# The relu of an index score stays in its PSUM bank, and a convolution is summed in a PSUM bank

## Chip, cores and metric

The kernel runs on one core of one Trainium2 chip. The metric is the device time of one execution in microseconds, the median of the runs shown.
The engines of the core are named as in the profile: PE (TensorE, matmuls), PEld (its weight loads), DVE (VectorE), ACT (ScalarE), POOL (GpSimd) and SP (which only issues DMAs here).
Each has its own list of instructions, fixed when the kernel is built, and runs it in that order: an instruction that waits holds up all that stand behind it on its engine.

## What is computed

The reference is a decoder of two layers over 512 tokens of width 1024, in fp32. Each layer has a mixer of four head groups (HGRN2, DSA, NSA, mLSTM), a cross attention and a SwiGLU. The change touches two places.

DSA's index picks 128 keys for each query by a score that sums relu'd products over eight heads:

```
rel = relu(einsum('bthd,bsd->bhts', iqb, ik))
score = einsum('bhts,bth->bts', rel, iwb)
score = where(causal, score, -inf);  _, idx = top_k(score, topk)
```

mLSTM's queries and keys come from a causal convolution of four taps along the tokens, and a silu:

```
qk = silu(causal_conv(qk, conv_w, conv_b));  q, k = split(qk, 2)
```

## The kernel before

Activations stand with features or tokens on the 128 partitions and 512 or fewer columns in the free dimension. Every fp32 matmul against a weight is made of three (high times high, low times high, high times low: L294 to L296 and L304 to L306). The weights come by DMA from SP into `wr`, ACT rounds them to `wh` (L285) and POOL subtracts to `wl` (L286, a two-input subtraction over 128x512).

A layer has three stages, and each opens its own PSUM banks. In the first, which the change is in, the banks are `acc` (two, from a pool that lives throughout), `tp`, `dt`, `o` and `mb` (one each) and `sc` (two). The first stage weaves together generators: DSA's index and selection (`dsa`), NSA (`nsa`, which mixes its attention and its compressed branch `nsa_cmp`), mLSTM (`ml`) and the input projections. Each `yield` gives a cost, and the shares in `COST` set in which order the instructions are recorded; a scheduler then sets the order on each engine by a timeline of its own. The order is thus not written in the code, and any change of buffers can move instructions that it does not name.

DSA's index, for each block of 128 queries from the second on (`tb` 1 to 3): two rounds of transposes give `iqT` (L458, in bank `dt`), and for each of eight heads a matmul writes scores into bank `dt` (L644; the alias maps `sc` and `tp` of this pool to `dt`), ACT writes the relu to an SBUF tile `rel` of a tag with four buffers (L646), and DVE adds it, times the head's weight, to `iacc` in SBUF (L649 and L650 for the first head, L653 for the others). `iacc` has one buffer. Sixteen rounds of MAX8 and MATCH_REPLACE8 (L661, L662) then select the 128 best in place, and L665 turns the result into a mask.

Bank `dt` has a single buffer and is shared with `nsa_cmp`: the transposes of `n_hid` (L1165), the product with `hT` (L1173), and others go through it.

mLSTM's convolution of one 128-feature chunk (`conv`) is an ACT instruction that writes tap 0 and the bias to `m_y` (L971), three DVE instructions that each add a tap (L973; inputs `m_x` and `m_y`, both in SBUF), a tanh on ACT (L975), the product of the silu on DVE (L977) and a split in high and low (L980 on ACT, then `m_lo` on POOL). It is called four times in a layer. Bank `mb` serves mLSTM's transposes (L957, and L458 with `mb`), its scores (L1013) and its values (L1030).

`nsa_cmp` runs twice over the same steps, once for keys and once for values: DVE gathers `n_blk` (L1145), adds the positions, splits it into `n_bs` (L1150 and a subtraction at the helper's line L316), and PE multiplies `n_bs` with 64 streamed weights (L1157) into an `acc` bank.

Of the kernel before, what the change touches and what calls it, by code (L numbers as in the profile page):

```python
# [15 lines left out]
D, S, MEM, DEPTH, FF = 1024, 512, 256, 2, 2816  # L16
# [186 lines left out]
class Kernel:  # L203
# [403 lines left out]
    def dsa(self, pool, keep):  # L607
        nc = self.nc
        idx = self.d_idx
        st = self.t(pool, "d_st", [128, 64], bufs=1)  # L610

        ik = idx[:, :, 256:288]
        self.sumsq(st[:, 4:8], ik, pool)
        self.rsqrt(pool, st[:, 8:12], st[:, 4:8], 1.0 / 32, EPS)
        self.tt(ik, ik, st[:, 8:12, None].to_broadcast([128, TB, 32]), OP.mult)
        self.tt(ik, ik, self.row("idxk_gain")[:, None, :].to_broadcast([128, TB, 32]), OP.mult)
        self.rope(idx[:, :, 256:288].rearrange("p t (h d) -> p t h d", h=1), self.ic, self.isn, 4, pool)
        iq = idx[:, :, 0:256].rearrange("p t (h d) -> p t h d", h=8)
        self.rope(iq, self.ic, self.isn, 4, pool)
        iks = self.t2(pool, "iks", [128, TB, 96], FR)  # L620
        nc.vector.tensor_copy(iks[:, :, 0:32], ik)
        nc.vector.tensor_copy(iks[:, :, 32:64], ik)
        self.tt(iks[:, :, 64:96], ik, iks[:, :, 0:32].bitcast(FT), OP.subtract)
        ikT = self.t(pool, "ikT", [128, S], FR, bufs=1)
        self.transpose_blocks(ikT[0:96], lambda j: iks[:, j, :].bitcast(FT), TB, nc.vector.tensor_copy, rows=96,
                              pool=pool)

        yield 4.0

        def index(tb):  # L630
            n = (tb + 1) * 128
            iqs = self.t(pool, "iqs", [128, 8, 96], FR, bufs=1)
            nc.scalar.activation(iqs[:, :, 0:32], iq[:, tb], AF.Copy)
            nc.scalar.activation(iqs[:, :, 64:96], iq[:, tb], AF.Copy)
            self.tt(iqs[:, :, 32:64], iq[:, tb], iqs[:, :, 0:32].bitcast(FT), OP.subtract, nc.gpsimd)
            iqT = self.t(pool, "iqT", [128, 8, 128], FR, bufs=1)
            for g in range(2):
                self.transpose_blocks(iqT[0:96, 4 * g:4 * g + 4].rearrange("p a b -> p (a b)"),
                                      lambda j: iqs[:, 4 * g + j, :].bitcast(FT), 4, self.act_copy, rows=96,
                                      pool=pool)  # L640
            acc = self.t(pool, "iacc", [128, S], bufs=1)[:, :n]
            for h in range(8):
                sc = self.psum("sc", pool=pool)
                nc.tensor.matmul(sc[:, :n], iqT[0:96, h], ikT[0:96, :n], start=True, stop=True)  # L644
                rel = self.t2(pool, "rel", [128, S])
                nc.scalar.activation(rel[:, :n], sc[:, :n], AF.Relu, scale=1.0 / 16)  # L646
                w = idx[:, tb, 288 + h:289 + h]
                if h == 0:
                    nc.vector.tensor_scalar(acc[:, :n - 128], rel[:, :n - 128], w, None, op0=OP.mult)  # L649
                    nc.vector.scalar_tensor_tensor(acc[:, n - 128:n], rel[:, n - 128:n], w, self.k("neg"),  # L650
                                                   op0=OP.mult, op1=OP.add)
                else:
                    nc.vector.scalar_tensor_tensor(acc, rel[:, :n], w, acc, op0=OP.mult, op1=OP.add)  # L653
                yield 0.7
            return acc

        def select(tb, acc, masks):
            n = (tb + 1) * 128
            m8 = self.t(pool, "m8", [128, 8])
            for r in range(16):  # L660
                nc.vector.max(m8, acc)  # L661
                nc.vector.match_replace(acc, m8, acc, -3e38)  # L662
                yield 0.4 + 0.25 * tb
            masks[tb] = self.t(keep, f"dmask{tb}", [128, n], BF, bufs=1)
            nc.vector.tensor_scalar(masks[tb], acc, -2e38, NEG, op0=OP.is_gt, op1=OP.mult)  # L665

        masks = self.d_masks = {0: None}
        for tb in range(1, TB):
            acc = yield from index(tb)
            yield from select(tb, acc, masks)  # L670
# [262 lines left out]
    def ml(self, pool):  # L933
# [33 lines left out]

        def conv(c):
            x = self.m_x[c]
            y = self.t2(pool, "m_y", [128, S])  # L970
            nc.scalar.activation(y, x[:, 0:S], AF.Identity, scale=self.col("conv_w", 4 * c), bias=self.col("conv_b", c))  # L971
            for j in range(1, 4):
                nc.vector.scalar_tensor_tensor(y, x[:, j:j + S], self.col("conv_w", 4 * c + j), y, op0=OP.mult, op1=OP.add)  # L973
            th = self.t2(pool, "m_th", [128, S])
            nc.scalar.activation(th, y, AF.Tanh, scale=0.5)  # L975
            z = th
            nc.vector.scalar_tensor_tensor(z, th, 1.0, y, op0=OP.add, op1=OP.mult)  # L977
            hi = self.t(pool, f"m_hi{c // 2}", [128, S], FR, bufs=1)
            lo = pool.tile([128, S], FR, name="m_lo", tag="m_x", bufs=4)
            nc.scalar.activation(hi, z, AF.Copy)  # L980
            self.tt(lo, z, hi.bitcast(FT), OP.subtract, nc.gpsimd)
            return hi, lo
# [10 lines left out]
        for h in range(4):  # L993
            po = 64 * (h % 2)
            if h % 2 == 0:
                while h and self.m_have < 2:
                    yield 0.2
                q = conv(h // 2)
                yield 3.0
                k = conv(2 + h // 2)  # L1000
                yield 3.0
# [6 lines left out]
            for sb in range(TB):  # L1008
                n = S - sb * 128
                sc = self.psum("mb")  # L1010
# [580 lines left out]
```

## Time and profile before

| what | value |
|---|---|
| median of 3 runs | 1689.46 us (1688.78 to 1691.2) |
| profiled execution | 1689.36 us, span 1687.6 us |
| mean granted TensorE clock | 0.973 of full speed |
| busy share of the span | PE 95%, PEld 79%, DVE 56%, POOL 47%, ACT 42% |
| first stage of layer 0 | from about 45 to 273 us |
| first stage of layer 1 | from about 884 to 1109 us |

The span begins with the first profiled instruction; 1.8 us of the execution lie outside it. Times in the text without another word are microseconds from the span's start in the profiled execution. A share of busy time is a mean over stages with different limits, so the stage of the change is read by itself.

### The profile page before, as it was taken

How to read it: one execution, taken by the hardware profiler on the slowest of the kernel's cores; microseconds unless marked ns; L12 is line 12 of the kernel's file. 1: busy time of each engine (PE TensorE's matmuls, PEld its weight loads, DVE VectorE, ACT ScalarE, POOL GpSimd, SP SyncE). 2: the span in 40 equal slices, each digit the busy share in tenths (PEclk: the TensorE clock that was granted, in tenths of full speed). 3: DMA queues.
4: the chain of work that ended last, by engine and by line, in shares of the span. 5: the costliest groups of instructions: out<-in, count | busy, mean ns of one | idle time of the engine just before them, and what ended most of it. 6: DMA issues, size and time to landing. Idle time of an engine off the chain costs nothing.

```text
span 1687.6 us, 25172 instructions
## 1 busy us (share of the span) xinstructions
PE 1608.2 (95%) x9256; PEld 1332.0 (79%) x9262; DVE 948.3 (56%) x1760; ACT 716.8 (42%) x1525; POOL 788.6 (47%) x698
## 2 busy tenths in 40 slices
PE   7899998998899999999998999889988999999999
PEld 7778877777788888888897787687867888888887
DVE  5697588875854421443227975887677644124420
ACT  5555453455653322333345654534555433223321
POOL 6554333456424444444456634244562344444442
PEclk9999997999999999999999999979999999999999
DMA  5342212213313333333232412022131233333332
GB/s 166 84 119 76 70 34 84 57 42 94 92 45 94 93 91 98 94 95 98 87 113 80 122 57 76 27 94 60 33 116 39 66 98 89 92 100 94 93 104 66
DMA packets 83259, 140.40 MB, mean 83 GB/s; under 512 B 9528, under 2 KB 24632, under 8 KB 83136
## 3 DMA queue, kind: packets, MB, share of 16 engines
q1 hardware_dynamic: 80784, 133.81, 27.2%
q10 hardware_dynamic: 2032, 3.94, 0.7%
q8 instruction: 73, 1.20, 0.3%
q0 software_dynamic: 320, 1.05, 0.2%
q14 instruction: 50, 0.41, 0.1%
HBM read 134.55 MB, written 4.21 MB: 82 GB/s over the span
## 4 chain that ended last, share of the span: by engine, by line
PE 79%; DVE 13%; issue 3%; ACT 2%; POOL 2%; DMA 1%; ACTq 0%; SPq 0%; POOLq 0%; DVEq 0%
PE acc L294 13%; PE acc L295 13%; PE acc L296 13%; PE sc L295 5%; PE sc L296 5%; PE sc L294 5%; PE hb L821 3%; PE acc L304 2%; PE acc L305 2%; PE acc L306 2%; PE o L539 2%; PE sc L517 2%; PE tp L458 2%; DVE m_y L973 1%; DVE iacc L662 1%
## 5 line engine op out<-in xcount | busy, mean ns | idle before, releaser
L286 POOL TENSOR_TENSOR wl<-wr,wh 128x512 fp32r<-128x512 f32 (+5 forms) x504 | 631.9, 1260 | 686.2 <-ACT wh L285 657.2
L285 ACT ACTIVATE wh<-wr 128x512 fp32r<-128x512 f32 (+5 forms) x504 | 297.1, 597 | 502.9 <-PE acc L295 209.9
L295 PE MATMUL acc<-xl,wh 128*128 128x512 f32 (+1 forms) x704 | 275.6, 392 | 3.3 <-DVE xl L1242 3.0
L294 PE MATMUL acc<-xh,wh 128*128 128x512 f32 (+1 forms) x704 | 276.3, 395 | 1.6 <-ACT xh L1248 1.1
L296 PE MATMUL acc<-xh,wl 128*128 128x512 f32 (+1 forms) x704 | 275.3, 391 | 2.5 <-POOL wl L286 2.5
L431 DVE TENSOR_TENSOR xT<-acc,xT 128x512 f32<-128x512 f32 (+1 forms) x112 | 68.0, 611 | 220.9 <-PE acc L296 220.3
L294 PEld LDWEIGHTS acc<-xh,wh 128*128 128x128 f32 x704 | 133.9, 191 | 34.0 <-DVE xT L431 2.1
L295 PEld LDWEIGHTS acc<-xl,wh 128*128 128x128 f32 x704 | 134.1, 190 | 32.2 <-DVE xl L1242 4.1
L296 PEld LDWEIGHTS acc<-xh,wl 128*128 128x128 f32 x704 | 134.1, 191 | 30.1 <-POOL wl L286 3.4
L304 PE MATMUL acc<-wh,xh 128*128 128x256 f32 (+2 forms) x480 | 139.8, 294 | 1.0 <-DVE xT L431 1.0
L305 PE MATMUL acc<-wl,xh 128*128 128x256 f32 (+2 forms) x480 | 138.3, 289 | 1.5 <-POOL wl L286 1.4
L295 PE MATMUL sc<-xl,wh 128*128 128x512 f32 x352 | 139.7, 397 | 0.0
L296 PE MATMUL sc<-xh,wl 128*128 128x512 f32 x352 | 138.9, 394 | 0.0
L296 PE MATMUL acc<-f_gh,wl 128*128 128x512 f32 x352 | 138.5, 395 | 0.0
L295 PE MATMUL acc<-f_gl,wh 128*128 128x512 f32 x352 | 138.4, 395 | 0.0
L294 PE MATMUL acc<-f_gh,wh 128*128 128x512 f32 x352 | 138.1, 394 | 0.0
L294 PE MATMUL sc<-xh,wh 128*128 128x512 f32 x352 | 138.0, 393 | 0.0
L306 PE MATMUL acc<-wh,xl 128*128 128x256 f32 (+2 forms) x480 | 136.9, 286 | 0.0
L1450 DVE SCALAR_TENSOR_TENSOR f_b<-sc,R 128x512 f32<-128x512 f32 x44 | 30.4, 690 | 127.5 <-PE sc L296 127.5
L304 PEld LDWEIGHTS acc<-wh,xh 128*128 128x128 f32 x480 | 91.9, 192 | 4.6 <-issue 2.1
L305 PEld LDWEIGHTS acc<-wl,xh 128*128 128x128 f32 x480 | 92.6, 193 | 3.0 <-POOL wl L286 2.0
L306 PEld LDWEIGHTS acc<-wh,xl 128*128 128x128 f32 x480 | 92.3, 192 | 0.1
(405 smaller groups left out, 3068.8 us busy)
## 6 DMA issues: line engine op xcount, KB each, us to landing
wr<-in_wst SPq DMA_DIRECT2D x384, 256.0 KB, 2.6
wr<-in_wst SPq DMA_DIRECT2D x48, 128.0 KB, 2.1
wr<-in_wst SPq DMA_DIRECT2D x32, 192.0 KB, 2.4
wr<-in_wst SPq DMA_DIRECT2D x16, 262.0 KB, 2.7
wr<-in_wst SPq DMA_DIRECT2D x16, 148.0 KB, 2.2
wr<-in_wst SPq DMA_DIRECT2D x8, 264.0 KB, 2.9
m_Mb<-m_dram ACTq DMA_DIRECT2D x8, 256.0 KB, 3.3
memT<-in_memT SPq DMA_DIRECT2D x16, 128.0 KB, 2.0
```

The source lines that it names most:

```text
L285: nc.scalar.activation(hi, raw, AF.Copy)
L286: nc.gpsimd.tensor_tensor(lo, raw, hi.bitcast(FT), op=OP.subtract)
L294: self.nc.tensor.matmul(acc, wh, xh, start=(j == 0), stop=False)
L295: self.nc.tensor.matmul(acc, wh, xl, start=False, stop=False)
L296: self.nc.tensor.matmul(acc, wl, xh, start=False, stop=(j == n - 1))
L304: self.nc.tensor.matmul(acc, xh[:, s], wh, start=(first and j == 0), stop=False)
L305: self.nc.tensor.matmul(acc, xh[:, s], wl, start=False, stop=False)
L306: self.nc.tensor.matmul(acc, xl[:, s], wh, start=False, stop=(last and j == n - 1))
L431: self.nc.vector.tensor_add(self.xT[c][:, cols], acc, self.xT[c][:, cols])
L458: self.nc.tensor.transpose(p[:rows, j * 128:j * 128 + 128], src(j), self.ident)
L517: nc.tensor.matmul(sc[:, e], q[j][:, h0 + e], job["kst"][:, :n], start=(j == 0), stop=False, skip_group_check=True)
L821: nc.tensor.matmul(sc[s0:s1, b + t0:b + t1], kk[po:po + 64, b + s0:b + s1], qq[po:po + 64, b + t0:b + t1], start=True, stop=True)
```

## The change

Two lines. `rel` no longer is a tile of its own: the relu is written back over the scores in their `dt` bank, and DVE reads them there, so the bank comes free only when L650 or L653 of that head has run. And `m_y` becomes a tile of bank `mb`: ACT writes tap 0 there, DVE adds the three taps there in place, and the bank comes free when L977 has read it.

```diff
             for h in range(8):
                 sc = self.psum("sc", pool=pool)
                 nc.tensor.matmul(sc[:, :n], iqT[0:96, h], ikT[0:96, :n], start=True, stop=True)
-                rel = self.t2(pool, "rel", [128, S])
+                rel = sc
                 nc.scalar.activation(rel[:, :n], sc[:, :n], AF.Relu, scale=1.0 / 16)
...
             x = self.m_x[c]
-            y = self.t2(pool, "m_y", [128, S])
+            y = self.psum("mb")
             nc.scalar.activation(y, x[:, 0:S], AF.Identity, scale=self.col("conv_w", 4 * c), bias=self.col("conv_b", c))
```

The scheduler lays the lists out anew. Three places in layer 0 are shown; in layer 1 the same happens.

PE, before, where the index of `tb` 1 ends: its last head is the L644 with 128x256, the transposes of `iqs` for `tb` 2 follow within a few instructions, and then the first head of `tb` 2 (L644 with 128x384).

```order
L644 MATMUL dt<-ikT,iqT 128x256
L305 MATMUL acc<-wl,xh 128x264
L306 MATMUL acc<-wh,xl 128x264
L458 MATMUL tp<-kc,ks 128x128 x4
L458 MATMUL dt<-kc,iqs 96x128 x4
L486 MATMUL tp<-kc,qd 128x128 x4
L458 MATMUL mb<-kc,m_g 4x128 x4
L458 MATMUL dt<-kc,iqs 96x128 x4
L517 MATMUL sc<-n_kst_767,qh 128x128
L517 MATMUL sc<-n_kst_846,qh 128x128
L644 MATMUL dt<-ikT,iqT 128x384
L1157 MATMUL acc<-wh,n_bs 64x256
```

PE, now, at the same place: the two last heads of `tb` 1, and directly behind them the first product of `nsa_cmp` with its 64 weights.

```order
L644 MATMUL dt<-ikT,iqT 128x256
L486 MATMUL tp<-kc,qd 128x128 x4
L458 MATMUL mb<-kc,m_g 4x128 x4
L644 MATMUL dt<-ikT,iqT 128x256
L1157 MATMUL acc<-wh,n_bs 64x256
L1157 MATMUL acc<-wl,n_bs 64x256
```

The transposes of `iqs` now stand some 100 and 140 instructions further on, and the first head of `tb` 2 another 30 behind them.

DVE, before, around the end of the selection of `tb` 1 (L665): `n_blk` and `n_bs` of the second run of `nsa_cmp` stand ahead of L665, the first head of `tb` 2 (L649, L650) behind it.

```order
L1145 COPY n_blk<-n_kv 64x16x31 x2
L1092 COPY qd<-n_qr 128x8x16
L316 TENSOR_TENSOR n_hs<-dt,n_hs 128x64
L662 MATCH_REPLACE iacc<-m_830,iacc 128x256
L316 TENSOR_TENSOR n_blk<-n_blk,cols 128x16x31
L661 MAX m_830<-iacc 128x8
L1150 CAST n_bs<-n_blk 128x16x32
L662 MATCH_REPLACE iacc<-m_830,iacc 128x256
L316 TENSOR_TENSOR n_bs<-n_blk,n_bs 128x16x32
L665 TENSOR_SCALAR dmask_1180<-iacc 128x256
L438 TENSOR_TENSOR m_x<-acc,R 128x512
L649 TENSOR_SCALAR iacc<-rel,d_idx 128x256
```

DVE, now, at the same place: the taps of the first convolution (L973) are around L665, and `n_blk` and `n_bs` come behind L665 and the first head.

```order
L665 TENSOR_SCALAR dmask_1172<-iacc 128x256
L973 SCALAR_TENSOR_TENSOR mb<-m_x,cols,mb 128x512
L649 TENSOR_SCALAR iacc<-dt,d_idx 128x256
L650 SCALAR_TENSOR_TENSOR iacc<-dt,d_idx,kc 128x128
L973 SCALAR_TENSOR_TENSOR mb<-m_x,cols,mb 128x512
L1145 COPY n_blk<-n_kv 64x16x31 x2
L1092 COPY qd<-n_qr 128x8x16
L316 TENSOR_TENSOR n_hs<-dt,n_hs 128x64
L316 TENSOR_TENSOR n_blk<-n_blk,cols 128x16x31
L977 SCALAR_TENSOR_TENSOR m_th<-m_th,mb 128x512
L1150 CAST n_bs<-n_blk 128x16x32
L316 TENSOR_TENSOR n_bs<-n_blk,n_bs 128x16x32
```

What moved: mLSTM's rows up to the first convolution went ahead of `n_bs`, and `n_hs`, which reads bank `dt`, went behind the first head of `tb` 2.

PE, before, at the last head of the index of `tb` 3 (the L644 with 128x512), with mLSTM's scores behind it:

```order
L644 MATMUL dt<-ikT,iqT 128x512
L1013 MATMUL mb<-m_hi_2749,m_hi_2803 128x384
L1013 MATMUL mb<-m_lo,m_hi_2803 128x384
L1013 MATMUL mb<-m_hi_2749,m_lo 128x384
L539 MATMUL o<-PT,n_tok 64x128 x7
```

PE, now, at the same head:

```order
L1013 MATMUL mb<-m_hi_2725,m_hi_2779 128x256
L1013 MATMUL mb<-m_lo,m_hi_2779 128x256
L1013 MATMUL mb<-m_hi_2725,m_lo 128x256
L458 MATMUL tp<-kc,P 128x128 x4
L644 MATMUL dt<-ikT,iqT 128x512
L458 MATMUL tp<-kc,P 128x128 x4
```

The head stands 25 instructions further on: behind the scores with 128x256, which followed it before.

## Rows read from the trace of the kernel before

**Rows 1.** The page's part 1: busy us, share of the span, instructions of each engine.
```profile
PE 1608.2 (95%) x9256; PEld 1332.0 (79%) x9262; DVE 948.3 (56%) x1760; ACT 716.8 (42%) x1525; POOL 788.6 (47%) x698
```

**Rows 2.** The page's part 4: the chain that ended last, by engine.
```profile
PE 79%; DVE 13%; issue 3%; ACT 2%; POOL 2%; DMA 1%; ACTq 0%; SPq 0%; POOLq 0%; DVEq 0%
```

**Rows 3.** Windows: stretch, length, busy of PE PEld DVE ACT POOL, PEclk, DMA, GB/s.
```profile
48.40:83.48 35.08, 27.82 (x196) 24.87 (x194) 27.00 (x55) 19.33 (x41) 22.44 (x17) 0.98 0.27 76
83.48:111.25 27.77, 25.43 (x159) 21.61 (x158) 23.87 (x66) 16.59 (x46) 16.24 (x14) 0.91 0.39 107
...
111.25:143.97 32.72, 31.70 (x242) 27.29 (x242) 27.52 (x40) 21.60 (x52) 20.23 (x16) 0.95 0.32 96
143.97:238.43 94.46, 94.29 (x594) 75.13 (x592) 68.82 (x146) 46.27 (x104) 34.95 (x27) 1.00 0.23 66
238.43:242.60 4.17, 4.17 (x33) 2.53 (x32) 3.59 (x8) 1.77 (x5) 0.00 (x0) 1.00 0.20 64
...
111.25:121.48 10.23, 9.67 (x71) 8.34 (x71) 10.20 (x17) 4.21 (x8) 5.72 (x4) 0.83 0.32 98
...
920.90:948.36 27.46, 24.91 (x158) 20.94 (x158) 24.37 (x66) 16.48 (x46) 16.08 (x14) 0.94 0.39 107
```

**Rows 4.** Waits of PE from 45 to 240: us in total, times, longest us.
```profile
PE dt L458 <- ACT rel L646: 3.1, 1, 3.1
PE dt L644 <- ACT iqT L462: 2.6, 1, 2.6
PE acc L1157 <- DVE n_bs L316: 2.3, 1, 2.3
```

**Rows 5.** Instructions of tiles `rel`, `m_y`, `mb`: ns min/median/max, first and last start, forms.
```profile
L646 ACT ACTIVATE rel<-dt x48: 362/488/598, 50.4 to 1076.0; 128x256 f32<-128x256 f32 x16, 128x384 f32<-128x384 f32 x16, 128x512 f32<-128x512 f32 x16
L653 DVE SCALAR_TENSOR_TENSOR iacc<-rel,d_idx,iacc x42: 472/746/1774, 53.9 to 1077.2; 128x256 f32<-128x256 f32 x14, 128x384 f32<-128x384 f32 x14, 128x512 f32<-128x512 f32 x14
...
L973 DVE SCALAR_TENSOR_TENSOR m_y<-m_x,cols,m_y x24: 736/1117/1810, 121.7 to 1064.1; 128x512 f32<-128x512 f32 x24
...
L977 DVE SCALAR_TENSOR_TENSOR m_th<-m_th,m_y x8: 683/942/1380, 127.2 to 1066.6; 128x512 f32<-128x512 f32 x8
...
L1021 DVE SCALAR_TENSOR_TENSOR m_p<-mb,m_d x32: 278/485/693, 162.5 to 1099.6; 128x512 f32<-128x512 f32 x8, 128x384 f32<-128x384 f32 x8, 128x256 f32<-128x256 f32 x8, 128x128 f32<-128x128 f32 x8
```

**Rows 6.** Timeline of DVE, 58 to 140: start us, us, instruction.
```profile
63.06 1.51 DVE L653 SCALAR_TENSOR_TENSOR iacc<-rel,d_idx,iacc 128x256 f32<-128x256 f32 x1
...
72.35 1.50 DVE L653 SCALAR_TENSOR_TENSOR iacc<-rel,d_idx,iacc 128x256 f32<-128x256 f32 x1
...
76.51 1.33 DVE L653 SCALAR_TENSOR_TENSOR iacc<-rel,d_idx,iacc 128x256 f32<-128x256 f32 x1 [0.28 <-ACT rel L646]
...
105.72 1.41 DVE L1092 COPY qd<-n_qr 128x128 f32<-128x128 f32 x1
...
107.52 1.28 DVE L316 TENSOR_TENSOR n_blk<-n_blk,cols 128x496 f32<-128x496 f32 x1
...
109.06 1.14 DVE L1150 CAST n_bs<-n_blk 128x512 fp32r<-128x512 f32 x1
...
110.52 0.68 DVE L316 TENSOR_TENSOR n_bs<-n_blk,n_bs 128x512 fp32r<-128x512 f32 x1
```

**Rows 7.** Timeline of DVE at the end of the stage, 205 to 280.
```profile
240.14 0.74 DVE L653 SCALAR_TENSOR_TENSOR iacc<-rel,d_idx,iacc 128x512 f32<-128x512 f32 x1
...
241.54 0.42 DVE L316 TENSOR_TENSOR mo<-o,spread 128x256 f32<-128x256 f32 x1
241.88 0.68 DVE L521 TENSOR_REDUCE stat<-sc 128x1 f32<-128x512 f32 x1
...
243.32 0.42 DVE L1021 SCALAR_TENSOR_TENSOR m_p<-mb,m_d 128x256 f32<-128x256 f32 x1
...
244.38 0.29 DVE L1021 SCALAR_TENSOR_TENSOR m_p<-mb,m_d 128x128 f32<-128x128 f32 x1
...
272.53 0.43 DVE L665 TENSOR_SCALAR dmask<-iacc 128x512 bf16<-128x512 f32 x1
```

## The prediction

> **What bounds the kernel now.** I read the page's shares first, then the chain by engine, then windows of the stage that the change is in, then the waits of PE there, and last DVE's timeline.
> PE is busy for 95% of the span [rows 1], and the chain that ended last runs 79% on PE and 13% on DVE [rows 2]. So time is won or lost only where PE stands still. The windows say where: from 48.40, where the first stage of layer 0 has its first NSA projection, to 111.25 PE is busy for 27.82 + 25.43 = 53.25 of 62.85 us and loses 9.6; from there to 238.43 it loses 1.0 + 0.2 more, 10.8 in all [rows 3]. In the first two windows DVE is busy for 27.00 of 35.08 and 23.87 of 27.77 us, mostly without a pause. The waits behind PE's loss are few [rows 4]: 3.1 and 2.6 us around the transposes for the index of `tb` 2, and 2.3 us at 111.25, where the second run of `nsa_cmp` waits for `n_bs`. At the end the stage hangs on DVE: the last L653 of the index starts at 240.14, and the selection behind it ends with L665 at 272.53 + 0.43 = 272.96 [rows 7]. Layer 1 repeats it (24.91 busy of 27.46 us before its `n_bs`, [rows 3]), so I work out one layer and double it.
>
> **What the operands cost.** The three taps and L653 have two inputs in SBUF, and their durations spread: L973 736 to 1810 ns, median 1117; L653 472 to 1774, median 746; L977 683 to 1380, median 942. L1021, the same operation with one input in a PSUM bank, never took more than 693 ns and has a median of 485 over its four widths [rows 5]. Long ones are those that overlap a POOL subtraction. With one input in PSUM I take L1021's longest, 0.69 us, for a tap and for L977 at 512 columns, and 0.42 us for a 256-column L653, as L1021 of that width in [rows 7].
> [...]
> What no row shows is a DVE write into PSUM, as the taps now do it. It lies between L977's least, 0.68, and L973's longest, 1.81, if contention stays; I take 0.69. ACT's write of the relu into PSUM I leave at L646's 0.36 to 0.60 us: ACT is busy for 42% [rows 1] and the difference would be hidden.
> By the medians DVE sheds in a layer 12 x (1.12 - 0.69) for the taps, 4 x (0.94 - 0.69) for L977 and 21 x (0.75 - 0.49) for L653: 5.2 + 1.0 + 5.5 = 11.7 us. That is no gain in time by itself; what counts is what PE waits for.
>
> **Step 1, the early waits.** PE's list now has the transposes of `iqs` some 100 and 140 instructions later, so 3.1 + 2.6 = 5.7 us of waits [rows 4] go. What is late next: bank `dt` now comes free only after L653 of the head before. In the index of `tb` 1 the sixth L653 ended at 72.35 + 1.50 = 73.85 [rows 6]; in the new list it stands behind `n_qr`, the copies into `qd` and the gathers, and I put the wait of the last head at 2.7 us and that for `n_bs` of the first run behind it at 1.8, together 4.5 (bounds 0 and 7). PE had lost 35.08 - 27.82 = 7.3 us by 83.48 [rows 3]; it now has lost 7.3 - 5.7 + 4.5 = 6.1.
>
> **Step 2, the second run of `nsa_cmp`.** Its first L1157 stands 37 instructions further on PE's list. Up to it PE has 53.25 us of work before [rows 3]; 355 instructions make 0.15 us each, so 37 add 5.5: 58.8. PE is there at 48.4 + 58.8 + 6.1 = 113.3.
> `n_bs` was ready at 110.52 + 0.68 = 111.2 [rows 6]. DVE's list now has ahead of it nearly all that ran from 111.25 to 121.48 (10.2 us busy, [rows 3]; 0.8 for a copy and one L653 stay behind it), three small copies of 0.4, and the first convolution, 4 x 0.69 = 2.8: 12.6 us more. Gone is the contention of three L653 in the index of `tb` 1: 1.51 + 1.50 + 1.33 - 3 x 0.42 = 3.1 [rows 6]. So `n_bs` is ready at 111.2 + 12.6 - 3.1 = 120.7. A lower bound: the copy into `qd`, `n_blk` and the cast into `n_bs` took 1.41, 1.28 and 1.14 under contention [rows 6]; if PE's standing also stops the weights that POOL prepares, they take the 0.68 of the subtraction beside them, 1.8 less: 118.9. I take the middle, 119.8, since some of the weights will still be in hand.
> So PE stands for 119.8 - 113.3 = 6.5 us before this L1157, mostly already at L1165 and the `qd` transposes ahead of it, which wait for bank `dt` (held from the first L644 of `tb` 2 until L650, which needs `iacc` free, so L665 done) and for `qd`. Queued behind are the 64 L1157, the next heads and mLSTM's value projection. PE's loss up to there is 119.8 - 48.4 - 58.8 = 12.6 us against the 10.8 that it had lost by 238.43: 1.8 us worse. From there PE has work without a pause as before (94.29 busy of 94.46 us, [rows 3]), with DVE at 68.82 of it, so I add nothing.
>
> **Step 3, the end of the stage.** The last head of the index of `tb` 3 stands 25 instructions further on: where it now is, before had got at 242.60 instead of 238.43, and PE was busy all through [rows 3]. That is 4.2 us. Given back: of what DVE ran during the last selection, instructions of 0.42, 0.68, 0.42 and 0.29 us [rows 7] now come before it: 1.8. Net 2.4 us worse.
>
> **Sum.** 1.8 + 2.4 = 4.2 us a layer, 8.4 in two. Against the profiled execution of 1689.36 (span 1687.6 and 1.8 around it, 0.1 under the median) that is 1697.8; I predict 1698. Its own range, with step 2 from 0.9 (at 118.9) to 2.7 (at 120.7) and 2 us either way in a layer for what the new order does elsewhere, is 1692 to 1704.
>
> **Rivals.**
> Faster: DVE's relief decides. If DVE gets to `n_bs` by 113.3, before PE needs it, nothing replaces the waits of step 1: PE's loss is 6.1, 4.7 under before, and with step 3's 2.4 a layer gains 2.3 us: 1684.8; without the 4.5 of new waits 6.8: 1675.8. For it speak the 11.7 us that DVE sheds; against it, that only 3.1 of them and the convolution's own fall ahead of `n_bs`, while 12.6 us of work move there. [...]
> No change: step 2 takes back what step 3 costs. That needs a loss of 10.8 - 2.4 = 8.4, so `n_bs` at 115.6, 4.2 us earlier than I put it: 1689.4.
> Slower by more: bank `dt` at every head. Each L644 now waits for a chain of its own matmul, ACT's relu (0.36 to 0.60) and L653 of the head before (0.42 to 0.69), some 1.6 us with the hand-overs. In `tb` 2 and 3 the heads stand 12 to 44 instructions apart, 1.8 to 6.6 us at 0.15, so a chain alone fits; but where L653 stands in DVE's list behind other work, PE pays. At 5 us a layer from the point where DVE is more than a head behind: 1697.8 + 10 = 1708.
> The change does not do what it says: DVE still waits for POOL with one input in PSUM. Then the 3.1 us stay and the convolution takes 3 x 1.12 + 0.94 = 4.3 instead of 2.8: 4.6 a layer, 1707.0. L1021's narrow spread speaks against it.
>
> **How the numbers follow.** Forecast 0.42, faster 0.23, no change 0.15, `dt` at every head 0.13, contention stays 0.07. The least that the measurement can tell from no change is about 0.2%, 3.4 us, and the cases fall on their sides of it: faster 0.23, same 0.15, slower 0.62. For 8 in 10 the range leaves out half of the faster case, its far end, and the outer part of the slow ones: 1681 to 1710.
>
> **What would show it.** Right: L973 and L653 near 0.69 and 0.42 to 0.69 with little spread; no wait of PE for ACT's relu near 76; instead a stand of some 6 us between 113 and 120 before L1165, the `qd` transposes or L1157, by bank `dt` or by DVE; the last L665 of layer 0 near 277, of layer 1 some 8 us later than before. Wrong: L665 at or before 273; PE without a stand over 3 us near 115; L973 still at 1.1 us or more; or a difference that arises after the first stage, in the attention, the cross attention or the feed-forward part, which I have taken as unchanged.

## The result, and the profile after

The changed kernel takes 1709.33 us (four runs, 1705.16 to 1711.0) against 1690.33 (1688.78 to 1694.39): a ratio of 1.0102, 95% interval 1.0082 to 1.0121. It is slower, as forecast, by 19.0 us where 8.4 were predicted; the time lies just inside the stated range of 1681 to 1710 us. Its profiled execution took 1711.0 us with a span of 1709.2, so the two traces differ by 21.6 us; of that 1.9 lie ahead of the first relu (52.30 against 50.42), where PE waits 10.9 instead of 8.8 us for its first `wh`. A later run in the same order, filled_stands, has its first relu at 50.51, so the order alone does not make these 1.9 us.

The page's part 1 of the changed kernel answers to [rows 1], its part 4 to [rows 2].

```profile
PE 1620.8 (95%) x9256; PEld 1342.2 (79%) x9262; DVE 924.6 (54%) x1760; ACT 720.8 (42%) x1525; POOL 779.1 (46%) x698
```

```profile
PE 81%; DVE 10%; issue 3%; POOL 2%; ACT 2%; DMA 1%; SPq 0%; ACTq 0%; POOLq 0%; DVEq 0%
```

PE executes the same 9256 instructions and is busy for 12.6 us longer. So more than half of the difference is no stand of PE: the same matmuls took longer, which I read as a lower granted clock (0.961 instead of 0.973 in the mean; an L1157 below takes 0.41 us at a granted clock of 0.50 and 0.28 at 1.00). DVE is busy for 23.7 us less: it did get the relief.

Now by stage. The windows run from the first L646 of a layer to the end of its last L665 (the first stage), and from there to the first L1450 (attention, output projection, cross attention: "the part behind"); first layer 0, then layer 1. The columns are as in [rows 3]. Before:

```profile
50.42:272.96 222.54, 203.54 (x1329) 166.37 (x1327) 179.68 (x389) 114.21 (x268) 96.00 (x74) 0.94 0.24 69
272.96:504.18 231.22, 216.00 (x1515) 181.75 (x1519) 163.66 (x321) 114.89 (x274) 116.29 (x122) 0.95 0.25 74
887.84:1109.68 221.84, 202.86 (x1331) 166.77 (x1330) 179.74 (x389) 114.16 (x268) 96.17 (x73) 0.95 0.25 69
1109.68:1337.01 227.33, 215.13 (x1515) 179.83 (x1518) 163.41 (x321) 113.70 (x275) 117.92 (x122) 0.97 0.24 70
```

After:

```profile
52.30:280.82 228.52, 206.17 (x1329) 170.55 (x1327) 165.50 (x389) 115.51 (x268) 92.02 (x74) 0.91 0.23 67
280.82:509.83 229.01, 214.37 (x1515) 179.57 (x1519) 162.94 (x321) 114.70 (x274) 116.52 (x122) 0.96 0.25 75
893.49:1121.15 227.66, 206.70 (x1330) 169.85 (x1329) 168.92 (x389) 116.68 (x270) 93.31 (x75) 0.91 0.23 67
1121.15:1358.61 237.46, 222.54 (x1515) 184.37 (x1518) 165.08 (x319) 114.16 (x272) 114.11 (x122) 0.94 0.22 67
```

The first stages are longer by 6.0 and 5.8 us, at a clock of 0.91 instead of 0.94 and 0.95. The part behind is shorter by 2.2 us in layer 0 and longer by 10.1 in layer 1, where the change touches nothing. What follows, the two feed-forward parts, is the same to 0.1 us. So the surprise is one window, the last: nearly half of the whole loss. There PE is busy for 222.54 instead of 215.13 us and idle for 14.9 instead of 12.2: 7.4 of the 10.1 us are longer work, 2.7 are stands.

**Inside the first stage.** The instructions of the two edits, by line: ns min/median/max. They answer to [rows 5].

```profile
L646 ACT ACTIVATE dt<-dt x48: 365/475/598, 52.3 to 1089.8; 128x256 f32<-128x256 f32 x16, 128x384 f32<-128x384 f32 x16, 128x512 f32<-128x512 f32 x16
L653 DVE SCALAR_TENSOR_TENSOR iacc<-dt,d_idx,iacc x42: 462/618/753, 57.8 to 1090.4; 128x256 f32<-128x256 f32 x14, 128x384 f32<-128x384 f32 x14, 128x512 f32<-128x512 f32 x14
L973 DVE SCALAR_TENSOR_TENSOR mb<-m_x,cols,mb x24: 741/749/757, 117.5 to 1071.1; 128x512 f32<-128x512 f32 x24
L977 DVE SCALAR_TENSOR_TENSOR m_th<-m_th,mb x8: 675/686/690, 122.6 to 1073.2; 128x512 f32<-128x512 f32 x8
```

The spread is gone: a tap takes 741 to 757 ns where it took 736 to 1810. ACT's relu has a median of 475 ns into PSUM, against 488 into SBUF before.

PE's waits from 45 to 145 us, us in total, times, longest; they answer to [rows 4]:

```profile
PE o L539 <- ACT PT L462: 3.5, 2, 2.8
PE mb L458 <- DVE m_g L316: 3.3, 1, 3.3
PE tp L486 <- DVE n_hs L316: 1.8, 1, 1.8
PE tp L486 <- DVE qd L1092: 1.1, 1, 1.1
PE dt L644 <- DVE iacc L653: 1.1, 2, 0.9
PE dt L1165 <- DVE iacc L650: 1.0, 1, 1.0
```

The three waits of [rows 4] are no longer among them; others stand in their place. The ones near 110 to 124 show in PE's timeline:

```profile
112.15 1.12 PE L539 MATMUL o<-PT,n_tok 128*64 128x128 f32 x8 [2.80 <-ACT PT L462]
...
119.85 0.48 PE L1165 MATMUL dt<-kc,n_hid 64*128 64x64 f32 x2 [1.02 <-DVE iacc L650]
122.09 1.08 PE L486 MATMUL tp<-kc,qd 128*128 128x128 f32 x4 [1.76 <-DVE n_hs L316]
...
124.64 0.41 PE L1157 MATMUL acc<-wl,n_bs 128*64 128x256 f32 x1
...
129.66 0.28 PE L1157 MATMUL acc<-wl,n_bs 128*64 128x256 f32 x1
```

and DVE's list around them answers to the last three of [rows 6]:

```profile
118.19 0.29 DVE L665 TENSOR_SCALAR dmask<-iacc 128x256 bf16<-128x256 f32 x1
...
119.45 0.34 DVE L650 SCALAR_TENSOR_TENSOR iacc<-dt,d_idx,kc 128x128 f32<-128x128 f32 x1
...
120.49 1.20 DVE L1145 COPY n_blk<-n_kv 64x496 f32<-64x496 f32 x2
...
123.62 0.69 DVE L316 TENSOR_TENSOR n_bs<-n_blk,n_bs 128x512 fp32r<-128x512 f32 x1
```

Read the two together: the first head of `tb` 2 holds bank `dt` until L650, L650 stands behind the end of the selection (L665), L1165 waits 1.0 us for the bank, and `n_blk` and `n_bs` stand behind L650 in DVE's list. `n_bs` is ready at 124.31 instead of 111.20. Which of the two makes it late, the held bank or the place in the list, the first experiment below decides. And look at the length of an L1157: 0.41 us at 124.64, 0.28 at 129.66, where the granted clock is 1.00 (from 128.70 to 131.00). Up to 128.70 it was lower:

```profile
50.30:85.38 35.08, 29.39 (x199) 26.93 (x198) 26.36 (x53) 19.13 (x40) 22.11 (x17) 0.94 0.26 76
85.38:124.37 38.99, 32.00 (x203) 26.32 (x201) 33.89 (x90) 20.87 (x59) 17.62 (x14) 0.81 0.32 95
...
111.60:128.70 17.10, 13.08 (x70) 11.22 (x71) 15.29 (x39) 10.48 (x25) 4.98 (x7) 0.50 0.18 55
```

From 111.60 to 128.70, from the end of the stand of 2.80 us on (109.35 to 112.15), PE's granted clock was 0.50. Its 13.08 us of work there would have taken 6.5 at a clock of 1.00, by an estimate of mine from the ratio of the two clocks; one L1157 starts 0.21 us behind the other there (124.64, 124.86), and 0.12 at 1.00 (129.54, 129.66).

### The profile page after: what moved, and what is told of

Read it like the earlier page. It is cut to its first block, busy times and chain, and to the rows that moved or that the text cites. A ratio compares the mean times of both kernels' runs of the same rounds, so it can differ in the third digit from the quotient of the medians.

```text
span 1709.2 us, 25147 instructions
## 1 busy us (share of the span) xinstructions
PE 1620.8 (95%) x9256; PEld 1342.2 (79%) x9262; DVE 924.6 (54%) x1760; ACT 720.8 (42%) x1525; POOL 779.1 (46%) x698
## 4 chain that ended last, share of the span: by engine, by line
PE 81%; DVE 10%; issue 3%; POOL 2%; ACT 2%; DMA 1%; SPq 0%; ACTq 0%; POOLq 0%; DVEq 0%
PE acc L294 14%; PE acc L295 14%; PE acc L296 13%; PE sc L295 5%; PE sc L296 5%; PE sc L294 5%; PE hb L821 3%; PE acc L304 3%; PE acc L305 2%; PE acc L306 2%; PE o L539 2%; PE sc L517 2%; PE tp L458 1%; DVE iacc L662 1%; POOL wl L286 1%
## 5 line engine op out<-in xcount | busy, mean ns | idle before, releaser
L1450 DVE SCALAR_TENSOR_TENSOR f_b<-sc,R 128x512 f32<-128x512 f32 x44 | 30.4, 691 | 127.5 <-PE sc L296 127.5
```

## Experiments

Two theories ran against each other at first. **Order theory:** the order that the scheduler made anew costs the time, the place of the operands does not. **Operand theory:** banks held longer, and DVE's writes into PSUM, cost it. To part them, a kernel can be given another kernel's order. All variants record the same instructions one by one before the scheduler sees them, so a table of places in that recording describes any order:

```diff
             Kernel(ctx, tc, i, o).run()
+            keep_order(nc, tc)
...
+def keep_order(nc, tc):
+    raw, at = zlib.decompress(base64.b85decode("".join(ORDER))), 0
...
+        for a, b in zip(order, order[1:]):
+            tc.add_manual_dep(mine[b], mine[a].name, dep(), reason="order")
```

Each instruction is tied to its predecessor on its engine; nothing else is added. Kernels with a table differ only in the table and in the lines named. That the tying costs nothing by itself is seen in old_late_new_order below: where it keeps the order of before, its windows are within 0.4 us of those of before.

The changed kernel and the twelve variants, with the medians; beside them the lengths of the four windows above less those of before, from each kernel's profiled execution (first stage and part behind of layer 0, then of layer 1):

| kernel | median us | ratio to before, 95% | stage 0 | behind 0 | stage 1 | behind 1 |
|---|---|---|---|---|---|---|
| changed | 1709.33 | 1.0102 (1.0082 to 1.0121) | +6.0 | -2.2 | +5.8 | +10.1 |
| old_ops_new_order | 1717.07 | 1.0155 (1.0135 to 1.0174) | +11.8 | -1.6 | +6.6 | +8.8 |
| new_late_old_order | 1706.48 | 1.0080 (1.0055 to 1.0105) | +5.5 | +6.0 | +7.0 | -1.7 |
| old_late_new_order | 1702.58 | 1.0071 (1.0055 to 1.0087) | +0.4 | -0.3 | +0.1 | +9.5 |
| relu_alone | 1711.91 | 1.0126 (1.0108 to 1.0143) | +10.2 | -0.4 | +10.1 | +2.1 |
| conv_alone | 1679.23 | 0.9917 (0.9887 to 0.9947) | -2.4 | -6.1 | -1.1 | -2.7 |
| relu_heads_2_to_8 | 1696.54 | 1.0024 (1.0006 to 1.0043) | -0.4 | +5.5 | +2.1 | +3.6 |
| first_head_sbuf | 1701.03 | 1.0053 (1.0037 to 1.0070) | +2.5 | +3.4 | +2.5 | +4.1 |
| iacc_two_buffers | 1696.16 | 1.0040 (1.0028 to 1.0052) | +4.6 | +1.5 | +0.2 | +0.4 |
| filled_stands | 1711.91 | 1.0112 (1.0073 to 1.0150) | +4.1 | -0.8 | +5.9 | +10.4 |
| old_ops_conv_order | 1686.43 | 0.9976 (0.9965 to 0.9987) | +1.8 | +3.7 | +0.6 | -2.3 |
| spliced_order | 1684.29 | 0.9970 (0.9960 to 0.9980) | +2.4 | -6.3 | +0.8 | -6.2 |
| old_ops_spliced_order | 1704.29 | 1.0088 (1.0076 to 1.0100) | +13.1 | -6.7 | +12.9 | -6.2 |

Each row of windows is one execution. In the same order the first stages repeat within 1.1 us (changed and new_late_old_order: 228.52 and 228.00, 227.66 and 228.79), but the part behind of layer 0 does not (229.01 and 237.24, see below). Some profiled executions lie far from the median of their kernel: relu_heads_2_to_8 took 1700.11 us in its profile, old_ops_conv_order 1694.94, the slowest of its twelve. The stretch ahead of the first relu, which is in no window, differs too: 50.4 us before, 53.6 in conv_alone, 55.4 in the two spliced kernels.

**Order or operands?** The first run takes the kernel before and gives it the changed kernel's order.

> The kernel before (relu in SBUF, convolution in SBUF), with every engine's instructions held in the order of the changed kernel. Order theory (the new order costs the time, the place of the operands does not): 1709 us like the changed kernel, from 1705 to 1716, with DVE's taps and L653 long again (1.1 and 0.75 us) and the half-clock stretch of 17 us from about 122 us still there. Operand theory (the banks held longer and DVE's writes into PSUM cost it): 1690 us, like before.

It took 1717.07 us, 7.7 more than the changed kernel and 1.1 above the range of the order theory. So in one and the same order the new places of the operands are a gain of 7.7 us, and the order is a loss of 26.3. The taps and L653 are back at their old spread:

```profile
L973 DVE SCALAR_TENSOR_TENSOR m_y<-m_x,cols,m_y x24: 735/750/1780, 115.6 to 1079.1; 128x512 f32<-128x512 f32 x24
...
L653 DVE SCALAR_TENSOR_TENSOR iacc<-rel,d_idx,iacc x42: 472/742/1785, 56.3 to 1096.1; 128x256 f32<-128x256 f32 x14, 128x384 f32<-128x384 f32 x14, 128x512 f32<-128x512 f32 x14
```

In this order the operand theory, as a cost, is dead. The expected median of 1.1 us for the taps was wrong: it is 0.75 in this order. The first three of layer 0 start from 115.61 to 117.65, while POOL stands idle (in the changed kernel, in the same order, it does so for 11.79 us up to 124.41), and take 0.75 us each.

This run also answers for the held bank. Here the relu is in SBUF, so no head holds `dt`, and L1165 does not wait:

```profile
116.82 0.47 PE L1165 MATMUL dt<-kc,n_hid 64*128 64x64 f32 x2
```

```profile
121.59 0.69 DVE L316 TENSOR_TENSOR n_bs<-n_blk,n_bs 128x512 fp32r<-128x512 f32 x1
```

Even so `n_bs` is ready 71.4 us after the first relu (122.28 - 50.84), against 72.0 in the changed kernel (124.31 - 52.30) and 60.8 before. From the first head of `tb` 2, the one that holds the bank, to `n_bs` it is 17.3 us here (122.28 - 105.01) and 17.2 in the changed kernel (124.31 - 107.11), in layer 1 18.1 and 18.2; the taps in between take 0.75 us in both. PE still loses 73.52 - 60.39 = 13.1 us up to its first L1157, and its granted clock is 0.54 from 109.70 to 126.60. So in the run it is the place in DVE's list, behind L665 and L650, that makes `n_bs` late, and not the bank.

**The window that nothing should have touched.** Two runs exchange the order of layer 1 behind its first stage, one into each kernel.

> The kernel before, with only the instructions of layer 1 behind its first stage put into the order of the changed kernel; no operand and nothing of either first stage is changed. Order theory: 1700 us (1696 to 1704), the 10 us appear behind 1109 us with a half-clock stretch. Rival, that the loss there comes from the changed first stage: 1690 us.

> The changed kernel, with the instructions of layer 1 behind its first stage put back into the order of the kernel before; all else in the new order. Order theory: the 10 us that layer 1 loses between 1109 and 1300 us go, 1699 us (1696 to 1703). Rival, that this loss is carried over from the first stage (later transfers, a lower clock) and not made by the order there: 1709 us.

Put into the kernel before, that piece of order costs 11.8 us (1702.58 against 1690.76), in the last window alone: +9.5 there, 0.4 or less in the three others. Taken out of the changed kernel, its last window falls from 237.46 to 225.64 us. The median of that run is nevertheless only 2.9 us lower, because in its profile the part behind of layer 0, whose order is untouched, took 237.24 us at a clock of 0.92, where the changed kernel's took 229.01 at 0.96:

```profile
280.31:517.55 237.24, 223.05 (x1515) 186.17 (x1519) 163.26 (x321) 114.27 (x274) 118.49 (x122) 0.92 0.24 72
...
1130.01:1355.65 225.64, 212.70 (x1508) 176.59 (x1511) 161.72 (x320) 112.50 (x272) 118.56 (x122) 0.98 0.23 71
```

Its six runs lie between 1697.19 and 1708.58 us: two under 1699 with a mean clock of 0.967 and 0.969, four above 1704 with 0.960 to 0.963. I take it that such a stretch comes in some executions and not in others; only a long one was profiled, and what starts it I have not shown. Part of what the piece of order does is seen in PE's waits there, of the changed kernel:

```profile
PE tp L1246 <- DVE h_g L316: 3.9, 2, 2.2
PE tp L458 <- ACT P L1387: 2.2, 1, 2.2
PE dt L688 <- DVE rs_ms L312: 1.5, 1, 1.5
```

The transposes of `h_g` stand twice, 3.9 us in all, and do not stand at all there before.

**Which of the two edits?**

> Only the relu is written back to its bank, the convolution stays in SBUF, the scheduler orders anew. Order theory: a new order, so the time can fall anywhere from 1688 to 1712, and the stand of PE before n_bs is small, since the convolution is not what the bank needs; my value 1697. Operand theory: bank dt held longer costs most of the 19 us: 1703 to 1709.

> Only the convolution is summed in its bank, the relu stays in SBUF; the scheduler orders anew. Hold theory: no hold of dt, so no stand of several us around 110 to 124; the first stages at 220 to 225 us as before; 1688 to 1700 us by how the order behind them falls. Theory of the prediction (the convolution ahead of n_bs): the stand is there, 1700 us or more.

```diff
-                rel = self.t2(pool, "rel", [128, S])
+                rel = sc
```

```diff
-            y = self.t2(pool, "m_y", [128, S])
+            y = self.psum("mb")
```

The relu alone loses 21.2 us, 10 in each first stage. The convolution alone gains 11.5 us by the medians, 9 to 19 by the ratio's interval: more than the 1688 to 1700 us that I had expected. The relu's PE waits, from 45 to 145 us, have one that towers:

```profile
PE dt L1165 <- DVE iacc L650: 6.1, 1, 6.1
PE mb L458 <- DVE m_g L316: 3.2, 1, 3.2
```

With the convolution alone they are those of before ([rows 4]: 3.1, 2.6, 2.3):

```profile
PE dt L458 <- ACT rel L646: 3.1, 1, 3.1
PE acc L1157 <- DVE n_bs L316: 2.1, 1, 2.1
PE dt L644 <- ACT iqT L462: 2.1, 1, 2.1
```

So the scheduler makes the order with the stand when the relu is in the bank, and not when the convolution alone is. With the convolution alone `n_bs` stands ahead of L665 and is ready at 113.77; with the relu alone it stands behind L650 and is ready at 127.53. I had expected 1697 for the relu alone, with a small stand; it took 1711.91 with the largest.

**Is it the hold of the bank?** Hold theory: bank `dt` stays taken by the first head of an index until the selection before has freed `iacc`, and that is what costs the time. Two ways to end the hold: the first head's relu in SBUF, or a second `iacc`.

```diff
-                rel = sc
+                rel = sc if h else self.t2(pool, "rel", [128, S])
```

```diff
-            acc = self.t(pool, "iacc", [128, S], bufs=1)[:, :n]
+            acc = self.t(pool, "iacc", [128, S], bufs=2)[:, :n]
```

> The changed kernel, except that the relu of the first head of each index goes to SBUF; the scheduler orders anew. Hold theory (bank dt is held by the first head until the selection before it has ended and frees iacc, and the transposes of n_hid wait for the bank, the slot of n_hid for them, n_blk and n_bs for the slot): PE's stands around 110 to 124 go, and the half-clock stretch there is at most 7 us; the first stage of each layer falls from 228 to 224 us or less; in all 1690 to 1702 us, since the order behind the first stage falls anew. Theory of the prediction (the convolution, which DVE's list puts ahead of n_bs, makes it late): the stands stay, 1705 to 1712 us.

> The changed kernel, with two buffers for iacc instead of one, so that the first head of an index need not wait for the selection before it; every relu still in bank dt; the scheduler orders anew. Hold theory: PE's wait at L1165 for L650 goes and each first stage falls by 4 us or more, to 224 us or less, as with the first head's relu in SBUF; in all 1690 to 1704 us by how the order behind the first stage falls. If the bank held by the other heads is what costs: the first stages stay at 227 to 229 us.

Both are faster than the changed kernel, by 8.3 and 13.2 us. In both the wait of L1165 for L650 is gone. With the first head in SBUF `n_bs` is ready at 117.74 instead of 124.31, with a second `iacc` at 124.43, as late as in the changed kernel; the first two lines are of first_head_sbuf, the third of iacc_two_buffers:

```profile
109.99 0.47 PE L1165 MATMUL dt<-kc,n_hid 64*128 64x64 f32 x2 [1.08 <-ACT rel L646]
```

```profile
117.06 0.68 DVE L316 TENSOR_TENSOR n_bs<-n_blk,n_bs 128x512 fp32r<-128x512 f32 x1
```

```profile
123.75 0.68 DVE L316 TENSOR_TENSOR n_bs<-n_blk,n_bs 128x512 fp32r<-128x512 f32 x1
```

The first stages fell from +6.0 and +5.8 to +2.5 and +2.5, and to +4.6 and +0.2. That is less than expected in three of four, and the half-clock stretch stayed (13 to 17 us in layer 0, where the mean clock of the first stage is 0.91 in both): PE still stands, 2.7 us at L539 with two `iacc`, 1.8 at the transposes behind `spread` and 1.1 at L1165 with the first head in SBUF, and DVE's list still has mLSTM's rows ahead of `n_bs`. Both kernels were ordered anew, so the 1.4 to 5.6 us that a first stage gained are not the hold's alone. Together with old_ops_new_order, where no bank is held and `n_bs` is as late, the hold as a cost in the run is not borne out; that it leads the scheduler to the bad order is likely, but not shown.

The relu without its first head can also be held in exactly the order of before, with the convolution left in SBUF:

> The kernel before, in exactly its own order; only the relu of heads 2 to 8 of each index goes back to its bank, the first head's relu stays in SBUF, the convolution too. If the place of the operand costs nothing and the order costs (order theory): 1684 to 1691 us, L653 near 0.42 us at 256 columns. If a bank held until DVE has read it costs time by itself: 1694 us or more, with PE waiting at L644 for L653.

It took 1696.54 us, ratio 1.0024 (1.0006 to 1.0043), and PE does wait for L653 (L644 4.1 us, L458 3.2, up to 145 us): the number and the wait of the second expectation. But the first stage of layer 0, where those waits are, loses nothing (-0.4), and that of layer 1 2.1 us. In the profiled execution, which is 3.6 us above the median, 5.5 and 3.6 us lie in the parts behind, in layer 0 at a lower clock (0.91 against 0.95) under an unchanged order. So what the held bank costs by itself stays open.

**What does the clock cost?** Clock theory: kept at work where it stands, PE keeps its clock.

```diff
             ph = self.psum("acc", (128, 256))
+            if s == 1:
+                for n in FILL:
+                    self.fill.append([nc.tensor.matmul(ph[:64], self.ikT[0:96, 0:64], self.ikT[0:96, 0:256], start=True, stop=True).ins
+                                      for _ in range(n)])
...
+FILL = (18, 8, 13)
```

> The changed kernel in its own order, with 39 matmuls of 64x256 more in each layer, written into the acc bank of the second run of nsa_cmp before its own first product: 18 ahead of the L539, 8 ahead of the L1165 and 13 ahead of the L486 that PE stands at between 108 and 124 us. Their results are overwritten. Clock theory (the stands of 6 us cost little by themselves, but the clock falls behind them and PE works at half speed for 17 us): PE no longer stands there, the 17 us at half clock go or shrink to 7 or less in both layers: 1709 minus 2 times 5 to 8, 1693 to 1700 us. If the clock falls for another reason: 1709 to 1713 us.

The clock held at the L1157 (now L1162), which take 0.28 us from the second on, but not at all of the added matmuls (L1156): the first 18 took 4.19 us, 0.23 each, the last 13 1.70, 0.13 each. The mean clock of the two first stages is 0.94 and 0.93, against 0.91 in both of the changed kernel.

```profile
106.94 4.19 PE L1156 MATMUL acc<-ikT 96*64 96x256 f32 x18
111.06 1.12 PE L540 MATMUL o<-PT,n_tok 128*64 128x128 f32 x8
...
115.91 1.15 PE L1156 MATMUL acc<-ikT 96*64 96x256 f32 x8
...
118.16 1.70 PE L1156 MATMUL acc<-ikT 96*64 96x256 f32 x13
...
122.46 0.33 PE L1162 MATMUL acc<-wh,n_bs 128*64 128x256 f32 x1 [0.53 <-DVE n_bs L317]
122.63 0.28 PE L1162 MATMUL acc<-wl,n_bs 128*64 128x256 f32 x1
```

The time did not fall: 1711.91 us (1704.13 to 1721.55), and the first stages are 1.9 us shorter and 0.1 longer than the changed kernel's (226.61 and 227.71 us), not 5 to 8 shorter. The first L1162 starts 72.0 us after the first relu, and `n_bs` of the changed kernel was ready after 72.0 too: up to there I read a slow PE as lying in the shadow of DVE. So filling the stands gave back at most 1.9 us of a stage: the clock theory failed as a lever.

**A better version.** The convolution alone beats both kernels. Is that its order or its operand?

> The kernel before (relu and convolution in SBUF) in the order that the scheduler made for the kernel with the convolution alone in its bank, which took 1679 us. Order theory: the 11 us came from that order, mostly from the part behind the first stages, so 1679 to 1684 us. Rival, that the convolution's place brought them: 1690 us or more.

1686.43 us, in neither of the two ranges: of the 11.5 us, by the medians, 7.2 are the operand's place (1686.43 - 1679.23) and about 4 the order. Last, the first stages of first_head_sbuf spliced with the parts behind of conv_alone:

> Relu of heads 2 to 8 and convolution in their banks, first head's relu in SBUF; first stages in the order of that kernel, all behind them in the order of the kernel with the convolution alone. By the two traces, against before: first stages -2.4 and -4.6 us, behind them -7.9 and -3.7 us, 1672 us if the parts add up (1669 to 1678). Rival, that the parts do not add up, because the clock behind a stage depends on what ran before it: 1679 us or more.

> The kernel before (relu and convolution in SBUF) in the same spliced order. The difference from the spliced kernel is the place of the operands alone. If that is worth what it was in the changed kernel's order (1717 against 1709): 7 us more than the spliced kernel. If the order is all: the same time within 2 us.

1684.29 us, the number of the rival but not its mechanism: the parts behind were taken over (-6.3 and -6.2), but the first stages came out at +2.4 and +0.8, not -2.4 and -4.6. Those two numbers I had taken from how far PE's list had got when L665 ended, and PE had only run ahead; the stage's end is on DVE, and counted to there first_head_sbuf itself has +2.5 and +2.5. Another 4.9 us lie ahead of the first relu, at 55.36 instead of 50.42, which I had not counted. With the old operands the same order takes 1704.29: the places of the operands are worth 20.0 us there, neither 7 nor nothing. The convolution alone, 1679.23 us, stays the fastest.

## Why the prediction was too low

**What the operands cost: right in kind.** The contention, the long times beside POOL, went, as forecast: the taps take 0.75 us (0.69 predicted), L977 0.69 (0.69), L653 at most 0.75. DVE sheds 14.2 and 10.8 us in the two first stages (11.7 predicted). In the trace of the kernel before all 14 taps over 0.8 us (898 to 1810 ns) overlap a TENSOR_TENSOR of POOL; of the ten others (736 to 752 ns) eight do. Now the 15 taps that overlap one take 742 to 757 ns, and the nine others 741 to 755. So L973 and L977, which spread from 736 to 1810 and from 683 to 1380 ns, now stay within 16 and 15 ns of their least. L977 and L653, which read PSUM and write SBUF, are at their least 8 and 10 ns shorter than before (675 against 683, 462 against 472). A tap, which also writes PSUM, is 741 ns at its least, against 736 before and 716 in relu_alone, both in SBUF.

**Step 1, the early waits: the sum right, its places in part not.** PE lost 35.08 - 29.39 = 5.7 us up to 85.38, 6.1 predicted. The old waits went, as forecast. The new ones are 3.3 us for `m_g`, in a transpose just ahead of the last head of `tb` 1, 1.1 for `qd`, 1.1 for L653 and 0.2 for `n_bs`, where I had 2.7 at the last head and 1.8 for `n_bs`.

**Step 2, the second run of `nsa_cmp`: the stand and its reason right, its price wrong.** Up to the first L1157 PE lost 5.69 + 6.99 = 12.7 us; 12.6 predicted. That the two agree is luck: `n_bs` came at 124.31 (119.8 predicted, 121.7 with the late start), 2.6 us later than I had it, and PE's work up to there was longer by as much, 61.39 us instead of 58.8. And I priced the stand as idle time alone. The clock was 0.50 from 111.60 on for 17 us, and the first stage lost 6.0 and 5.8 us where step 2 and step 3 together gave 4.2. For the reason I put the work that DVE's list has ahead of `n_bs` first and the bank second. The run with the old operands in the new order bears that out: no bank is held there, and `n_bs` is as late. What I had not seen is where that list comes from: the convolution that I named in it does not bring it about (conv_alone has no such stand), while both kernels with every relu in its bank and one `iacc` have it.

**Step 3, the end: right.** The last L653 starts at 250.52, L665 ends at 280.82: 30.30 us instead of 32.82, so 2.5 given back, 1.8 predicted. Counted by PE's instructions, the one that ends at 230 in the kernel before ends 5.8 us later now, 1.9 of it from the start; so 3.9 of the stage's 6.0 us were lost by then, and 2.1 arose here, 2.4 predicted. Of the 3.9, 2.1 are stands of PE (1.8 predicted in step 2) and 1.8 longer work of the same 1132 matmuls, which step 2 had not priced.

**The sum: the step that failed** is its silent term, "I have taken as unchanged" for what lies behind the first stage; only the range had 2 us either way in a layer for what the new order does elsewhere. The prediction itself names a difference there as its last sign of being wrong. It measured -2.2 in layer 0, which is within what executions of one order differ by, and +10.1 in layer 1, and old_late_new_order shows that the order there does the latter by itself, with old operands and old first stages: 11.8 us by the medians. I had seen that the scheduler lays all lists out anew and had read the new lists only where the change is. With this term at 7.9, the first stages at 11.8 instead of 8.4, and 1.9 at the start, the sum is the 21.6 of the two profiles.

**The rivals.** Faster: DVE did shed what it said, and at a fixed order this was worth 7.7 us; it lost to the order. `dt` at every head: its time, 1708, was met by luck and its mechanism was not; PE's waits for L653 come to 1.1 us up to 145, where relu_heads_2_to_8, in the old order, has 7.3. Contention stays: refuted, no tap took more than 757 ns. No change: the condition was `n_bs` by 115.6, and it came at 124.31.

**What stays open:** what makes the granted clock fall in some executions and not in others behind the first stage of layer 0, which under one and the same order made 8 us; and what in the relu's bank leads the scheduler to put `n_bs` late.

## What to carry to other kernels

When a scheduler lays out the whole program, a two-line change has two effects, one of the lines (7.7 us gained here) and one of the new order (26.3 us lost): compare the new lists in every stage before calling a stage unchanged, and part the two effects by giving one kernel the other's order. Before a bank is kept as a scratch tile, follow its release to the last reader and ask what that reader waits for: here the first of eight heads waited for an accumulator that a selection of 16 rounds still held. Taking that head out made the kernel 8.3 us faster than the changed one, but it stayed slower than the kernel before (ratio 1.0053). Read the granted clock behind a stand of PE as well: here it was 0.50 for 17 us, from the end of a stand of 2.80 us on. But where DVE set the next event, filling the stands gave at most 1.9 us of a stage back.

## What I had not expected of the hardware

What the place of operands is worth differs widely between orders: moving them out of SBUF gained 7.2 us in conv_alone's order (the convolution alone), 7.7 in the changed kernel's (both edits) and 20.0 in the spliced one (the convolution and the relu of heads 2 to 8). In the order of before, the relu of heads 2 to 8 alone lost some time by it (ratio 1.0024). That the gain goes by how much an order leans on DVE is my reading and not tested. In the spliced order, with the operands in SBUF, a tap has a median of 1.00 us and PE stands 5.2 us in one piece for ACT's `PT`:

```profile
L973 DVE SCALAR_TENSOR_TENSOR m_y<-m_x,cols,m_y x24: 729/1002/1794, 123.2 to 1085.8; 128x512 f32<-128x512 f32 x24
```

```profile
PE o L539 <- ACT PT L462: 5.2, 1, 5.2
```

DVE's accumulation in place in a PSUM bank is steady to 16 ns over 24 taps (741 to 757 ns), in a kernel whose POOL is busy for 46% of the span. And the half-clock stretch of 17 us, in which PE's work grew by 6.5 us by the estimate above, seems to have cost its stage less than that: with the stands filled, and the L1157 behind them at 0.28 us, the stage was 1.9 us shorter in one layer and no shorter in the other.
